# The latents' second FFN product as seven block products, with weight sums made by transfers that add into SBUF

## The chip, the cores and the metric

One core of one Trainium2 chip runs the whole program; seven cores are idle. The metric is the device time of one execution in microseconds (us), as the median of several runs. Engines are named as the profile names them: PE is TensorE (PEld its weight loads), DVE is VectorE, ACT is ScalarE, POOL is GpSimd, SP is SyncE, which only issues transfers here.

## The reference

Two layers of a diffusion backbone, on 1024 latent tokens and 256 context tokens of width 1024, in float32. Each layer has a mixer (attention on half of the heads, a spatial gate on the others) and then a SwiGLU FFN with 2816 hidden units:

```python
def swiglu(h, w_ffn_in, w_ffn_out):
    gate, up = jnp.split(h @ w_ffn_in, 2, axis=-1)
    return (jax.nn.silu(gate) * up) @ w_ffn_out
...
        fx = swiglu(modulate(rms_norm(x, g_pre_ffn[l]), mx[3], mx[4]), w_ffn_in[l], w_ffn_out[l])
        x = x + mx[5] * rms_norm(fx, g_post_ffn[l])
        if not last:
            fc = swiglu(modulate(rms_norm(xc, g_pre_ffn[l]), mc[3], mc[4]), w_ffn_in[l], w_ffn_out[l])
            xc = xc + mc[5] * rms_norm(fc, g_post_ffn[l])
```

The change concerns the last product of `swiglu` for the latents, (1024 x 2816) @ (2816 x 1024), in both layers. The vectors `mx` and `mc` come from six 1024 x 1024 products of the conditioning vectors with `w_mod` per layer.

## The kernel before, in words

A float32 product is made on PE as three products of float32r operands: each operand is split into a rounded part (`rnd`, an ACT copy) and a rest (`sub_lo`, a DVE subtraction of two SBUF operands), and high x high, high x low and low x high are summed in PSUM. So each 128 x 128 x 512 block of a product takes three matmuls and two splits that serve several blocks.

SBUF is handed out by rings: `PG` has 35 pages of 4 KB per partition, `BG` four buffers of 16 KB, `BK` the eight PSUM banks. Each engine works its instructions in a fixed order; the scheduler of the framework lays it down when the program is built, from the order of the code and from priorities.

For each layer, in order: projections of the mixer (`pz`, `pkv`, `pq`), attention, output projection (`op`), then the latents' FFN, then in layer 0 the context's FFN (`ffn`).

- `ffn_in` makes the latents' hidden units. It is already a product in seven block products (Strassen-Winograd): POOL makes the block sums of the weights (`wsplit`), each of the products takes 12 matmuls into one PSUM bank (`product`), DVE and ACT combine. Hidden units go to DRAM as 22 tiles `hid[j]` of 128 units x 1024 tokens.
- `ffn_out` is the product that changes. It takes the 22 tiles in chunks of two to four. For a chunk, SP loads `hid[j]` and row block j of `w_fo` (512 KB each) into `BG`, ACT and DVE split them (`foh`, `fol`, 128 x 1024), and then for each of eight token tiles and each half of the output columns PE does three matmuls per j. DVE adds the result of a chunk to `acc` (L1264); ACT copies the first chunk there. A generator loads and splits the next chunk meanwhile.
- `mods_steps` are small jobs that make `mx` and `mc`: per job 8 loads of 512 KB of `w_mod`, 8 (or 16, for both vectors) multiply-adds of 128 x 1024 on DVE (L234) into `macc`, and a few matmuls `mg`. `fill(n)` takes n steps of the queued jobs at places where DVE has room. In layer 0, nine such jobs (`later`) are queued before the FFN and are worked off in `ffn_in` and `ffn_out` of layer 0; layer 1 has none.
- `post` (L1346 on) is the end for a token tile: add the last partial sums (L1352), squares on ACT, `rsqrt` on POOL, scale on DVE (L1373), add the residual (L1374), store. In layer 1 it is called by `l_fin` for each token tile in the last chunk, and its last instance ends the program.

Of the kernel before, what the change touches and what calls it, by code (L numbers as in the profile page):

```python
# [10 lines left out]
F32 = mybir.dt.float32  # L11
F32R = mybir.dt.float32r
# [83 lines left out]
def trunk(ctx: ExitStack, tc, x, xctx, w_mod, b_mod, vecs, gqk, gsg, g_post, w_z, w_in, w_sT, w_out,  # L96
# [418 lines left out]
    def layer(l):  # L515
        nonlocal xl_d, xc_d
        last = l == DEPTH - 1
        hT = HT()
# [51 lines left out]
        for g, (kind, prs) in enumerate(groups):  # L570
            upages[g] = [PG.get([2 * len(prs), PC], F32, "u") for _ in range(2)]
            for k, pr in enumerate(prs):
# [634 lines left out]
        def ffn_out(done, hook, fills, chunks):  # L1207
            acc = []
            parts = {}
            starts = [sum(chunks[:i]) for i in range(len(chunks) + 1)]  # L1210

            def load(c):
                n = chunks[c]
                raws = []
                for k in range(2):
                    b = BG.get([n, 1024], F32, "fo")
                    raws.append(shares(b, [b.t[:, i] for i in range(n)]))
                    for i in range(n):
                        j = starts[c] + i
                        dma(out=b.t[:, i], in_=w_fo[l, j * P:(j + 1) * P, :] if k else hid[j])  # L1220
                parts[c] = []
                for i in range(n):
                    res = []
                    for k in range(2):
                        hi, lo = PG.get([1024], F32R, "foh"), PG.get([1024], F32R, "fol")
                        rnd(hi.t, raws[k][i].t)
                        sub_lo(lo.t, raws[k][i].t, hi.t)
                        raws[k][i].free()
                        res.append((hi, lo))
                    parts[c].append(res)  # L1230
                    yield

            def run():
                for c, n in enumerate(chunks):
                    first, final = c == 0, c == len(chunks) - 1
                    nxt = iter(()) if final else load(c + 1)
                    if first:
                        for _ in range(2):
                            b = BG.get([4, 1024], F32, "acc")
                            acc.extend(shares(b, [b.t[:, i] for i in range(4)]))  # L1240
                    if final:
                        hook()
                    for tt in range(NL):
                        if not final:
                            fill(fills)
                        sl = slice(tt * P, (tt + 1) * P)
                        bks = [BK.get([512], F32, "fo") for _ in range(2)]
                        for hs in (((0,), (1,)) if final and tt == NL - 1 else ((0, 1),)):
                            for i, ((hh, hl), (wh, wl)) in enumerate(parts[c]):
                                for k, (st_, mv) in enumerate(((hh, wh), (hh, wl), (hl, wh))):  # L1250
                                    for h in hs:
                                        mm(bks[h].t, st_.t[:, sl], mv.t[:, h * 512:(h + 1) * 512], i + k == 0,
                                           i == n - 1 and k == 2)
                        if tt > 0:
                            next(nxt, None)
                        if final:
                            done(tt, acc[tt], bks)
                            continue
# [275 lines left out]
```

## Time and profile before

| | |
|---|---|
| median of 3 runs | 2755.24 us (2754.25 to 2755.7) |
| the profiled execution's own time | 2754.34 us |
| its span (first to last instruction) | 2752.6 us, so 1.74 us lie around it |
| mean granted TensorE clock | 0.993 of full speed |
| PE busy | 2704.4 us, 98% |
| DVE, ACT, POOL busy | 72%, 45%, 16% |
| share of fo matmuls in the chain that ended last | 19.3% |

An engine's busy time is the time in which at least one of its instructions ran. Matmuls overlap in the pipeline, so the cost of one is read from the distance between starts, and not from its duration.

### The profile page before, as it was taken

To read this page: it belongs to the slowest core of one execution; us is meant where nothing else is said; L and a number is where in the kernel's file an instruction comes from. 1 tells how busy PE (TensorE), PEld (TensorE's weight loads), DVE (VectorE), ACT (ScalarE), POOL (GpSimd) and SP (SyncE) were. 2 spreads that over 40 slices of the span, in tenths; PEclk is the share of its full clock that TensorE was granted. 3 is DMA by queue.
4 is the path that set the end of the run, shared out by engine and by line. 5 is a ranking of instruction groups with operands and counts; after the bars stand their busy time and mean duration, and the time that the engine had idled before them with its cause. 6 is when DMAs were issued, how large, how long until landed. Compare 5 with 4: busy or idle time off the path is not lost.

```text
span 2752.6 us, 35200 instructions
## 1 busy us (share of the span) xinstructions
PE 2704.4 (98%) x13393; PEld 2216.6 (81%) x13393; DVE 1973.9 (72%) x2806; ACT 1234.4 (45%) x2073; POOL 435.6 (16%) x463
## 2 busy tenths in 40 slices
PE   7999999999999999999999999999998999999998
PEld 3789777688888788888899889777787888888887
DVE  6775878857888897865688556888758666666544
ACT  5323888845233223411276423788744333335111
POOL 1012000013233332000010002000013232330003
PEclk9999999999999999999999999999999999999999
DMA  7330000233532443742376410001232221225223
GB/s 283 123 117 32 9 10 26 78 111 108 210 128 107 153 144 132 257 170 98 105 240 224 146 56 32 5 9 39 93 126 92 85 80 66 92 77 191 85 77 115
DMA packets 91608, 298.04 MB, mean 108 GB/s; under 512 B 20431, under 2 KB 21263, under 8 KB 86318
## 3 DMA queue, kind: packets, MB, share of 16 engines
q1 hardware_dynamic: 91438, 295.78, 30.8%
q8 instruction: 105, 1.72, 0.3%
q14 instruction: 65, 0.53, 0.1%
HBM read 249.96 MB, written 45.71 MB: 107 GB/s over the span
## 4 chain that ended last, share of the span: by engine, by line
PE 88%; ACT 4%; DVE 3%; DMA 3%; issue 1%; POOL 1%; SPq 0%; DVEq 0%; POOLq 0%; ACTq 0%
PE fi_k L112 35%; PE fo_k L112 19%; PE op_k L112 7%; PE pz_k L112 6%; PE pv_k L112 6%; PE st_k L112 4%; PE pq_k L112 4%; PE pkv_k L112 2%; PE ml_k L112 2%; ACT pt_p L115 1%; ACT sp_b L118 1%; PE mg_k L112 1%; PE hT_k L334 1%; DMA wor_p<-in_w_out_dram 1%; PE m_k L112 1%
## 5 line engine op out<-in xcount | busy, mean ns | idle before, releaser
L112 PE MATMUL fi_k<-blk_p,fw_p 128*128 128x512 f32 x2640 | 608.6, 390 | 1.2 <-ACT blk_p L118 1.2
L112 PEld LDWEIGHTS fi_k<-blk_p,fw_p 128*128 128x128 f32 x2640 | 496.2, 188 | 106.3 <-ACT blk_p L118 2.1
L112 PE MATMUL pv_k<-sp_b,vt_p 128*128 128x512 f32 (+2 forms) x1008 | 277.6, 394 | 4.9 <-DVE sp_b L121 3.9
L118 ACT ACTIVATE fw_p<-fir_b 128x512 fp32r<-128x512 f32 x200 | 125.7, 631 | 317.6 <-PE fi_k L112 301.3
L112 PE MATMUL fi_k<-blk_b,fw_p 128*128 128x512 f32 x1056 | 251.0, 394 | 0.0
L112 PEld LDWEIGHTS fi_k<-blk_b,fw_p 128*128 128x128 f32 x1056 | 200.9, 191 | 42.3 <-DVE y_p L990 0.4
L286 POOL TENSOR_SCALAR rs<-ss 128x1 f32<-128x1 f32 x74 | 22.9, 309 | 1335.3 <-DVE ss L986 608.8
L121 DVE TENSOR_TENSOR sp_b<-pt_p,sp_b 128x1024 fp32r<-128x1024 f32 (+1 forms) x168 | 200.3, 1195 | 27.9 <-ACT sp_b L118 25.7
L112 PE MATMUL fo_k<-foh_p,foh_p 128*128 128x512 f32 x704 | 218.5, 390 | 0.0
L112 PE MATMUL fo_k<-fol_p,foh_p 128*128 128x512 f32 x704 | 218.0, 389 | 0.0
L112 PE MATMUL fo_k<-foh_p,fol_p 128*128 128x512 f32 x704 | 217.8, 389 | 0.0
L112 PEld LDWEIGHTS pv_k<-sp_b,vt_p 128*128 128x128 f32 (+1 forms) x1008 | 162.5, 170 | 63.0 <-DVE sp_b L121 11.0
L1264 DVE TENSOR_TENSOR acc_b<-fo_k,acc_b 128x512 f32<-128x512 f32 x176 | 113.1, 684 | 139.2 <-PE fo_k L112 139.1
L737 DVE TENSOR_REDUCE mx<-ml_k 128x1 f32<-128x512 f32 x256 | 168.0, 684 | 36.9 <-PE ml_k L112 36.3
L118 ACT ACTIVATE foh_p<-fo_b 128x1024 fp32r<-128x1024 f32 x88 | 90.8, 1060 | 226.9 <-PE fo_k L112 123.9
L115 ACT ACTIVATE pt_p<-st_k 128x512 f32<-128x512 f32 (+1 forms) x336 | 180.5, 590 | 14.4 <-PE st_k L112 13.3
L121 DVE TENSOR_TENSOR fw_p<-fir_b,fw_p 128x512 fp32r<-128x512 f32 x200 | 177.4, 887 | 11.8 <-ACT fw_p L118 9.6
L234 DVE SCALAR_TENSOR_TENSOR macc_p<-wm_p,cT,macc_p 128x1024 f32<-128x1024 f32 x128 | 171.8, 1357 | 13.7 <-DMA wm_p<-in_w_mod_dram 11.6
L118 ACT ACTIVATE sp_b<-pt_p 128x1024 fp32r<-128x1024 f32 (+1 forms) x168 | 175.8, 1047 | 1.7
L112 PE MATMUL pz_k<-winh_p,hTl_b 128*128 128x512 f32 x512 | 160.3, 391 | 1.0 <-DVE hTl_b L121 0.5
L112 PEld LDWEIGHTS fo_k<-foh_p,foh_p 128*128 128x128 f32 x704 | 131.8, 188 | 28.8 <-issue 0.9
L112 PEld LDWEIGHTS fo_k<-fol_p,foh_p 128*128 128x128 f32 x704 | 132.1, 188 | 27.7
(261 smaller groups left out, 5191.8 us busy)
## 6 DMA issues: line engine op xcount, KB each, us to landing
wm_p<-in_w_mod_dram SPq DMA_DIRECT2D x112, 512.0 KB
fir_b<-in_w_fi_dram SPq DMA_DIRECT2D x40, 1024.0 KB
fir_p<-in_w_fi_dram SPq DMA_DIRECT2D x52, 512.0 KB
hid<-hid_p SPq DMA_DIRECT2D x44, 512.0 KB
fo_b<-hid SPq DMA_DIRECT2D x44, 512.0 KB
fo_b<-in_w_fo_dram SPq DMA_DIRECT2D x44, 512.0 KB
for_p<-in_w_fo_dram SPq DMA_DIRECT2D x22, 512.0 KB
wraw_p<-in_w_z_dram SPq DMA_DIRECT2D x16, 512.0 KB
```

What stands on the lines that cost most here:

```text
L112: nc.tensor.matmul(o, lhsT, rhs, start=start, stop=stop)
L115: A.activation(out=o, in_=i, func=f, **kw)
L118: A.activation(out=o, in_=i, func=AF.Copy)
L121: V.tensor_tensor(out=o, in0=i, in1=hi.bitcast(F32), op=ALU.subtract)
L234: V.scalar_tensor_tensor(out=accs[v].t, in0=w.t, scalar=cT[:, v, kt:kt + 1], in1=accs[v].t, op0=ALU.mult, op1=ALU.add)
L286: nc.gpsimd.tensor_scalar(out=y, in0=src, scalar1=float(eps), scalar2=1.0, op0=ALU.add, op1=ALU.mult)
L334: nc.tensor.transpose(bk.t[:, k, :], xs.t[:, (4 * q + k) * P:(4 * q + k + 1) * P], idn)
L737: V.tensor_reduce(out=mx[:, b, i:i + 1], in_=bk.t, axis=AX.X, op=ALU.max)
L1264: V.tensor_tensor(out=a, in0=bks[h].t, in1=a, op=ALU.add)
```

## The change

`ffn_out` is written anew. Tokens are halved (512 each), output columns are halved (512 each), and the hidden tiles are halved by parity: `Hab` is token half a of the tiles `hid[2p + b - 1]`, and `Wab` is column half b of the row blocks 2p + a - 1 of `w_fo`, for p from 0 to 10. The product is made as seven block products, in the order 1, 2, 7, 6, 4, 5, 3. Each has 11 steps p, and a step is 4 token tiles x 3 matmuls into four PSUM banks. The operand of a step is split into pages `fs` (128 x 2 x 512). POOL makes the combinations of hidden blocks (`comb`, in products 7, 6, 5 and 3). The sums of weight blocks are made in place: a transfer issued by POOL (`nc.gpsimd.dma_start` with `accum_op`) adds a block from DRAM to the block that lies in SBUF (products 7, 6, 4 and 5). Preparation of a step runs `LEAD` = 6 steps ahead of its matmuls, sums are issued 4 steps ahead of the preparation, loads 7.

Two smaller edits come with it: the jobs (1, 2), (1, 3), (1, 4) of `w_mod` move from layer 0 to the mixer projections of layer 1, and (1, 5) to layer 1's FFN; and `post` adds only the banks that it is given, since half of the results are complete before. In layer 1, `post` of token tiles 4 to 7 runs after product 5, while product 3 is made.

```diff
     def layer(l):
         nonlocal xl_d, xc_d
         last = l == DEPTH - 1
+        jobs.extend(mods_steps(*a) for a in later[l][0])
...
-                    if kind == "l":
-                        fill(4)
+                if kind == "l":
+                    fill(4)
...
-                fill(0)
+                fill(2)
...
-        def ffn_out(done, hook, fills, chunks):
+        def ffn_out(done, hook):
...
+            steps = [(i, p) for i in (1, 2, 7, 6, 4, 5, 3) for p in range(NPR)]
...
+            needs = {1: ("H11", "W11"), 2: ("H12", "W21"), 7: ("H21", "W12"), 6: ("H22",), 4: (), 5: ("H11", "W11"),
+                     3: ("H12", "W22")}
+            sums = {7: ("W12", "W22"), 6: ("W12", "W11"), 4: ("W12", "W21"), 5: ("W11", "W12")}
...
+            def more_loads():
+                n = done_["prep"]
+                while todo_ and todo_[0][0] < n + AHEAD and (todo_[0][0] <= n or len(PG.queue) > 6):
+                    load()
+                while sums_ and sums_[0][0] < n + SUM and (sums_[0][1], sums_[0][3]) in raw:
+                    _, dst, src, p = sums_.pop(0)
+                    nc.gpsimd.dma_start(out=raw[dst, p].t, in_=block(src, p), accum_op=add_)
+
+            def comb(o, a, b, op):
+                nc.gpsimd.tensor_tensor(out=o.t, in0=a.t, in1=b.t, op=op)
...
+                for x_ in (h, w):
+                    t = PG.get([2, 512], F32R, "fs")
+                    rnd(t.t[:, 0], x_.t)
+                    sub_lo(t.t[:, 1], x_.t, t.t[:, 0])
+                    res.append(t)
...
+            def mms(bk, i, p, t):
+                h, w = split[i, p]
+                for k, (a, b) in enumerate(((0, 0), (0, 1), (1, 0))):
+                    mm(bk.t, h.t[:, a, t * P:(t + 1) * P], w.t[:, b], p + k == 0, p == NPR - 1 and k == 2)
...
+                    elif i == 6:
+                        V.tensor_tensor(out=z_, in0=bk.t, in1=z_, op=add_)
+                        V.tensor_tensor(out=x_, in0=bk.t, in1=x_, op=sub_)
...
-        if not last:
-            jobs.extend(mods_steps(*a) for a in later)
-        load_out, run_out = ffn_out(l_fin, before_c, 0 if last else 1, [2, 3, 3, 3, 3, 4, 4] if last else [2, 3, 3, 3, 3, 3, 2, 3])
+        jobs.extend(mods_steps(*a) for a in later[l][1])
+        c0, run_out = ffn_out(l_fin, before_c)
...
+    later = [((), [(0, 3, (1,)), (0, 4, (1,)), (0, 5, (0, 1)), (1, 0, (0, 1)), (1, 1, (0, 1))]),
+             ([(1, 2, (0,)), (1, 3, (0,)), (1, 4, (0,))], [(1, 5, (0,))])]
```

On POOL, the place between the last `wsplit` of layer 0's `ffn_in` and what follows. `fir` and `S` are weight tiles of `ffn_in`, `macc` the sums of a `w_mod` job, `rs` the `rsqrt` of a norm. Before:

```order
L1102 TENSOR_TENSOR fir_b_9076<-fir_b_9076 128x512
L1105 TENSOR_TENSOR fir_b_9076<-fir_b_9076,S_p_9451 128x512
L227 MEMSET macc_p_9726 128x1024
L227 MEMSET macc_p_10039 128x1024
L227 MEMSET macc_p_10388 128x1024
L286 TENSOR_SCALAR rs<-ss 128x1
```

After the change, where `fo` are raw blocks (DMA rows are the adding transfers, TENSOR_TENSOR rows the `comb`):

```order
L1106 TENSOR_TENSOR fir_b_9076<-fir_b_9076,S_p_9436 128x512
L1261 DMA fo_p_9903<-in_w_fo_dram 128x512 x2
L1261 DMA fo_p_9953<-in_w_fo_dram 128x512 x2
L1261 DMA fo_p_9996<-in_w_fo_dram 128x512
L1264 TENSOR_TENSOR fo_p_9901<-fo_b_9553,fo_p_9901 128x512 x2
L1261 DMA fo_p_9996<-in_w_fo_dram 128x512
L1261 DMA fo_p_10040<-in_w_fo_dram 128x512 x2
L1264 TENSOR_TENSOR fo_p_9951<-fo_b_9553,fo_p_9951 128x512 x2
L1261 DMA fo_p_10086<-in_w_fo_dram 128x512 x2
```

Three memsets gave way to a queue of adding transfers and combinations in turn; 44 of each stand there per layer, and a transfer that waits for its block holds up the combinations behind it.

On PE, the first instructions of layer 0's `ffn_out`. Before, two banks (column halves) and the tiles `foh`, `fol`; the numbers are those of buffers:

```order
L112 MATMUL fo_k711_9668<-foh_p739_9590,foh_p737_9586 128x512
L112 MATMUL fo_k712_9669<-foh_p739_9590,foh_p737_9586 128x512
L112 MATMUL fo_k711_9668<-fol_p740_9591,foh_p737_9586 128x512
L112 MATMUL fo_k712_9669<-fol_p740_9591,foh_p737_9586 128x512
L112 MATMUL fo_k711_9668<-foh_p739_9590,fol_p738_9587 128x512
```

After, four banks (token tiles), three matmuls each per step:

```order
L112 MATMUL fo_k711_9695<-fs_p729_9559,fs_p728_9556 128x512 x3
L112 MATMUL fo_k712_9696<-fs_p729_9559,fs_p728_9556 128x512 x3
L112 MATMUL fo_k713_9697<-fs_p729_9559,fs_p728_9556 128x512 x3
L112 MATMUL fo_k714_9698<-fs_p729_9559,fs_p728_9556 128x512 x3
L112 MATMUL fo_k711_9695<-fs_p731_9594,fs_p730_9591 128x512 x3
```

A new pair of `fs` pages is needed every 12 matmuls, and the banks change every 132.

On DVE, the place where layer 0 ends and layer 1's projections begin. `macc` and `wm` belong to the moved jobs, `acc` to the context's token tiles, `winl` are splits of the next projection weights. Before:

```order
L376 TENSOR_TENSOR winl_p1168_13738<-wraw_p1166_13735,winh_p1167_13737 128x1024
L1321 TENSOR_TENSOR acc_p908_11679<-fo_k945_13644,acc_p908_11679 128x512
L1321 TENSOR_TENSOR acc_p908_11679<-fo_k946_13645,acc_p908_11679 128x512
L376 TENSOR_TENSOR winl_p1165_13732<-wraw_p1163_13729,winh_p1164_13731 128x1024
L376 TENSOR_TENSOR winl_p1171_13744<-wraw_p1169_13741,winh_p1170_13743 128x1024
```

After:

```order
L234 SCALAR_TENSOR_TENSOR macc_p_13884<-wm_p_13956,cT,macc_p_13884 128x1024
L234 SCALAR_TENSOR_TENSOR macc_p_14085<-wm_p_14088,cT,macc_p_14085 128x1024
L234 SCALAR_TENSOR_TENSOR macc_p_13884<-wm_p_13959,cT,macc_p_13884 128x1024
L234 SCALAR_TENSOR_TENSOR macc_p_14085<-wm_p_14091,cT,macc_p_14085 128x1024
L234 SCALAR_TENSOR_TENSOR macc_p_13884<-wm_p_13962,cT,macc_p_13884 128x1024
L234 SCALAR_TENSOR_TENSOR macc_p_14085<-wm_p_14094,cT,macc_p_14085 128x1024
L234 SCALAR_TENSOR_TENSOR macc_p_14085<-wm_p_14097,cT,macc_p_14085 128x1024
L376 TENSOR_TENSOR winl_p_14103<-wraw_p_14100,winh_p_14102 128x1024
```

Of the 24 multiply-adds that moved to layer 1, the first twelve stand close together there (the last seven of them are shown), ahead of the splits `winl` of the gate's second projection and ahead of the two matmuls `mg` that PE reaches after 143 matmuls of the projection.

## Rows read from the trace of the kernel before

**Rows 1.** The page: span, busy time per engine, chain by engine.

```profile
span 2752.6 us, 35200 instructions
PE 2704.4 (98%) x13393; PEld 2216.6 (81%) x13393; DVE 1973.9 (72%) x2806; ACT 1234.4 (45%) x2073; POOL 435.6 (16%) x463
PE 88%; ACT 4%; DVE 3%; DMA 3%; issue 1%; POOL 1%; SPq 0%; DVEq 0%; POOLq 0%; ACTq 0%
```

**Rows 2.** Busy time in both FFN stages of each layer; instruction counts in brackets.

```profile
core 0: us, PE busy (x) PEld busy (x) DVE busy (x) ACT busy (x) POOL busy (x), PEclk, DMA share, GB/s
760.00:1109.00 349.00, 349.00 (x1560) 287.88 (x1559) 294.22 (x353) 106.75 (x174) 117.37 (x75) 0.99 0.38 133
1109.70:1358.60 248.90, 248.90 (x1113) 203.79 (x1112) 165.13 (x211) 59.35 (x69) 3.41 (x6) 1.00 0.42 152
1556.00:1700.00 144.00, 144.00 (x881) 129.18 (x880) 80.30 (x161) 46.23 (x97) 22.01 (x39) 1.00 0.16 54
2150.00:2504.00 354.00, 354.00 (x1564) 293.12 (x1563) 229.24 (x301) 115.81 (x185) 98.04 (x71) 1.00 0.22 84
2504.40:2744.00 239.60, 239.56 (x1057) 198.02 (x1056) 120.04 (x158) 57.90 (x85) 24.29 (x27) 1.00 0.33 120
```

**Rows 3.** The chain that ended last, layer 1's FFN: start, us, what.

```profile
2096.87 407.74 PE fi_k L112 x1797
2504.60 233.71 PE fo_k L112 x1031
```

**Rows 4.** PE's timeline at the step from `ffn_in` to `ffn_out`, layer 1.

```profile
2495.83 8.78 PE L112 MATMUL fi_k<-blk_p,fw_p 128*128 128x512 f32 x38
2504.44 0.62 PE L112 MATMUL fo_k<-foh_p,foh_p 128*128 128x512 f32 x2
2504.89 0.61 PE L112 MATMUL fo_k<-fol_p,foh_p 128*128 128x512 f32 x2
```

**Rows 5.** Groups by shape: busy us, mean ns, idle before and its releasers.

```profile
L118 ACT ACTIVATE fw_p<-fir_b 128x512 fp32r<-128x512 f32 x200 | 125.7, 631 | 317.6 <-PE fi_k L112 301.3 <-POOL fir_b L1102 6.6 <-DVE macc_p L234 4.2
L1264 DVE TENSOR_TENSOR acc_b<-fo_k,acc_b 128x512 f32<-128x512 f32 x176 | 113.1, 684 | 139.2 <-PE fo_k L112 139.1
L234 DVE SCALAR_TENSOR_TENSOR macc_p<-wm_p,cT,macc_p 128x1024 f32<-128x1024 f32 x128 | 171.8, 1357 | 13.7 <-DMA wm_p<-in_w_mod_dram 11.6 <-issue 1.2
L227 POOL MEMSET macc_p<- 128x1024 f32 x16 | 15.3, 954 | 147.4 <-DVE macc_p L234 55.2 <-PE fo_k L112 28.1 <-DVE winl_p L376 26.8
```

**Rows 6.** One tile's instructions: min/median/max ns (splits, POOL sums, SP issues).

```profile
L121 DVE TENSOR_TENSOR fw_p<-fir_b,fw_p x200: 673/692/1772, 705.2 to 2491.8; 128x512 fp32r<-128x512 f32 x100
L1100 POOL TENSOR_TENSOR S_p<-fir_b x40: 1277/1291/2225, 696.8 to 2471.3; 128x512 f32<-128x512 f32 x40
L1220 SPq DMA_DIRECT2D fo_b<-hid x44: 320/426/1396, 1059.6 to 2626.3; - x44
```

**Rows 7.** Timeline of DVE and POOL in layer 1's `ffn_in`.

```profile
2301.26 1.29 POOL L1101 TENSOR_TENSOR S_p<-S_p,fir_b 128x512 f32<-128x512 f32 x1
2301.36 1.74 DVE L121 TENSOR_TENSOR fw_p<-fir_b,fw_p 128x512 fp32r<-128x512 f32 x1
2302.51 1.75 POOL L1102 TENSOR_TENSOR fir_b<-fir_b 128x512 f32<-128x512 f32 x1
2303.03 1.78 DVE L1148 TENSOR_TENSOR hid_p<-hid_p,u_p 128x512 f32<-128x512 f32 x1
2304.73 0.68 DVE L1135 TENSOR_TENSOR u_p<-fi_k,u_p 128x512 f32<-128x512 f32 x1
2305.34 0.68 DVE L121 TENSOR_TENSOR fw_p<-fir_b,fw_p 128x512 fp32r<-128x512 f32 x1
```

**Rows 8.** Transfers: a busy stretch, and landings in the chain that ended last.

```profile
1120.00:1150.00 30.00, 30.00 (x134) 24.86 (x133) 26.68 (x25) 14.07 (x20) 1.91 (x2) 1.00 0.99 367
528.18 4.30 DMA wor_p<-in_w_out_dram
1540.84 6.23 DMA wraw_p<-in_w_z_dram
```

**Rows 9.** The end of the program: PE and DVE timeline.

```profile
2743.57 0.39 PE L112 MATMUL fo_k<-foh_p,fol_p 128*128 128x512 f32 x1
2744.19 0.68 DVE L1352 TENSOR_TENSOR acc_b<-fo_k,acc_b 128x512 f32<-128x512 f32 x1
2748.10 1.29 DVE L1374 TENSOR_TENSOR acc_b<-acc_b,x_p 128x512 f32<-128x512 f32 x2
```

More of the change, by code (lines that the diff above doesn't have):

```diff
@@ L1231, in load @@
                     yield
             def run():
[L1234 to L1241, printed above, removed]
-                        hook()
[L1243 to L1258, printed above, removed]
-                        for h in range(2):
-                            a = acc[tt].t[:, h * 512:(h + 1) * 512]
-                            if first:
-                                act(a, bks[h].t, AF.Copy)
-                            else:
-                                V.tensor_tensor(out=a, in0=bks[h].t, in1=a, op=ALU.add)
-                            bks[h].free()
-                    for _ in nxt:
-                        pass
-                    for res in parts.pop(c):
-                        for a in res:
-                            for b in a:
-                                b.free()
@@ L1273, in ffn_out @@
-            return load, run
+                for _ in range(2):
+                    b = BG.get([4, 1024], F32, "acc")
+                    acc.extend(shares(b, [b.t[:, k] for k in range(4)]))
+                half["acc"] = None
+                bks = None
+                for i, p in steps:
+                    more_loads()
+                    if ready_:
+                        prep()
+                    if (i, p) == ((4, 0) if last else (3, 0)):
+                        hook()
+                    if p == 0:
+                        bks = [BK.get([512], F32, "fo") for _ in range(4)]
+                    if i == 3 and p >= TM:
+                        if p == NPR - 1:
+                            for t in range(4):
+                                for q in range(TM, NPR):
+                                    mms(bks[t], 3, q, t)
+                                done(t, acc[t], [(1, bks[t])], t == 3)
+                            for q in range(TM, NPR):
+                                drop_split(3, q)
+                            if not last:
+                                for t in range(4, NL):
+                                    done(t, acc[t], [])
+                        continue
+                    for t in range(4):
+                        mms(bks[t], i, p, t)
+                    drop_split(i, p)
+                    if p == NPR - 1:
+                        evict(i, bks)
@@ L1275, in ffn @@
+            return begin(), run
         def ffn(h2v, T, done, cur, hook=None, tail=2, chores=()):
@@ L1351, in add @@
             def add(h):
-                V.tensor_tensor(out=acc.t[:, hs[h]], in0=bks[h].t, in1=acc.t[:, hs[h]], op=ALU.add)
-                bks[h].free()
+                for k, bk in bks:
+                    if k == h:
+                        V.tensor_tensor(out=acc.t[:, hs[h]], in0=bk.t, in1=acc.t[:, hs[h]], op=ALU.add)
+                        bk.free()
             if late:
@@ L1390, in layer, with l_fin @@
         chores, tails = [], []
-        def l_fin(tt, acc, bks):
+        def l_fin(tt, acc, bks, end=False):
             if last:
                 rest = post(acc, bks, xl_d[tt], cc["g_l"], out[tt * P:(tt + 1) * P, :],
-                            eng=V if tt == NL - 1 else nc.gpsimd)
+                            eng=V if end else nc.gpsimd)
                 next(rest)
@@ L1399, in l_fin @@
                 tails.append(rest)
-                if tt == NL - 1:
+                if end:
                     next(rest)
@@ L1426, in c_fin @@
         def c_fin(tt, acc, bks):
-            for _ in post(acc, bks, xc_d[tt], cc["g_c"], None):
+            for _ in post(acc, list(enumerate(bks)), xc_d[tt], cc["g_c"], None):
                 pass
@@ L1473, in trunk @@
         jobs.append(mods_steps(0, part, vs_))
-    later = [(0, 3, (1,)), (0, 4, (1,)), (0, 5, (0, 1)), (1, 0, (0, 1)), (1, 1, (0, 1)), (1, 2, (0,)), (1, 3, (0,)),
-             (1, 4, (0,)), (1, 5, (0,))]
+    later = [((), [(0, 3, (1,)), (0, 4, (1,)), (0, 5, (0, 1)), (1, 0, (0, 1)), (1, 1, (0, 1))]),
+             ([(1, 2, (0,)), (1, 3, (0,)), (1, 4, (0,))], [(1, 5, (0,))])]
     layer(0)
```

108 lines of the change are left out of this document (86 added, 22 removed).

## The prediction

> **What bounds the kernel now.** I read the page first: PE is busy for 98% of the span and holds 88% of the chain that ended last [rows 1]. An average says nothing of the stage that changes, so I then cut the span into stages. In both FFN stages of both layers PE is busy for the whole stretch at full clock: 248.90 of 248.90 us in layer 0's second product and 239.56 of 239.60 us in layer 1's, while DVE has work for 165 and 120 us and POOL for 3 and 24 us [rows 2]. The chain says the same: 233.71 us of it is one unbroken run of 1031 fo matmuls [rows 3]. So in this stage the end is set by the number of matmuls, and what is off PE has room.
>
> A matmul's own duration (0.39 us) is no price, since matmuls overlap. The price is the distance between starts: 38 matmuls from 2495.83 to 2504.44 make 0.2266 us each, two fo matmuls 0.45 us [rows 4]; the chain gives 233.71 / 1031 = 0.2267 us [rows 3]. The block products of `ffn_in` (the fi rows) have the loop that the change brings here (12 matmuls into a bank, a weight load for each), and they run at 407.74 / 1797 = 0.2269 us. The new loop therefore has the price of the old one.
>
> **What is removed.** Before, a layer has 22 tiles x 8 token tiles x 2 halves x 3 = 1056 matmuls. After, 7 products x 11 steps x 12 = 924. That is 132 fewer per layer and 264 in all: 264 x 0.2267 = 59.8 us. A step lasts 12 x 0.2267 = 2.72 us and the 77 steps of a layer 209.5 us. The matmuls `mg` of the four moved jobs are the same ones at another place where PE is also busy (the third of [rows 2]): 0. Layer 0's stage is 9.5 us longer than its 1056 matmuls (239.4 us); that is `mg` and transposes, which are kept or moved: 0.
>
> **What is added, per layer, against 209.5 us of PE.**
>
> ACT: two splits per step, 154 x 0.631 = 97 us [rows 5], and four copies. Hidden.
>
> DVE: 154 subtractions at the median 0.692 us [rows 6] = 106.6 us, and 28 additions from PSUM at 0.684 us [rows 5] = 19.2 us. Against this there is a collision: while POOL combines two SBUF tiles, a DVE instruction that reads two SBUF tiles takes 1.74 and 1.78 us in place of 0.68, and one that reads PSUM stays at 0.68 [rows 7]; the maximum of 200 splits is 1.772 us [rows 6]. So a combination holds up at most one such instruction by 1.08 us: 44 x 1.08 = 47.5 us at worst. Sum at most 173 us of 209.5. Hidden, and if this cover went (DVE over 209.5 us), every further us would be PE's.
>
> POOL: 44 combinations at 1.29 [rows 6] to 1.75 us [rows 7], say 1.5. And 44 adding transfers, of which no row exists. Their price on POOL is bounded below by what SP needs to issue a load, 0.43 us [rows 6], and above by POOL's shortest full-tile instruction, 0.954 us [rows 5], held up by three DVE instructions of 0.69 us, 3.03 us. I take 0.95, since it is POOL that must do the work and PSUM readers do not hold it. Is there time? The first sum is queued 4 steps ahead of preparation 22, when PE is at step 12; the last is for step 65, prepared when PE is at step 59. In those 47 steps (127.8 us) POOL has 33 combinations (49.5 us) and 44 sums. So 78.3 / 44 = 1.78 us per sum are free, and 2.15 us if the six steps of lead (16.3 us) are eaten too. At 0.95 us nothing waits.
>
> Landing: loads landed 4.30 to 6.23 us after issue for 512 KB [rows 8]. An adding transfer of 256 KB may take less, or twice that (12.5 us) if the add halves the rate. Four steps and six of lead allow 27.2 us. Hidden.
>
> Traffic: 121 loads and 44 sums of 256 KB are 43.3 MB in 209.5 us, 206 GB/s; with sums counted twice 262 GB/s. 367 GB/s were moved over 30 us [rows 8]. Hidden, if the short rows of 2 KB don't cost more than the 4 KB rows of that stretch.
>
> At one point a page speaks against this. First the row: only DVE instructions with two SBUF inputs were held, and by one POOL instruction each [rows 7]. The Trainium skill, page "SBUF — State Buffer", section "SBUF: two separate sides", calls the port pair that POOL and DVE share an exclusive lock, which a DVE instruction with two SBUF inputs takes only against a POOL instruction that reads SBUF; the trace agrees for combinations (1.74 us). By that rule the splits don't hold up the writing of descriptors, and the sum stays as it is. The same page tells of a transfer issued by POOL that took some 3.1 us in place of 0.62 beside a DVE copy in a two-port mode; if that held here, my estimate from its figure would be 44 x (3.1 - 2.15) = 42 us of waiting per layer, and the time about 2783. No run here shows it yet.
>
> **The moved jobs.** 24 multiply-adds of 1.357 us [rows 5] go to layer 1's projections, where DVE is busy for 80 of 144 us and PE for all of it [rows 2]. The first twelve (16.3 us) stand close together ahead of the first `mg`, which PE reaches after 143 matmuls, 32 us in. They fit, if their loads land; the context's last work and one landing of 6.23 us [rows 8] take most of the rest. Between 0 and 16.3 us; I take 2. What is late next would be the splits `winl`, which PE needs 43 us in.
>
> **The ends.** The last matmul starts at 2743.57 and the span ends 9 us later, through add, square, `rsqrt`, scale, add, store [rows 9]. This chain is kept. Four tiles are finished earlier, but the last four have 15 matmuls (3.4 us) each in place of 24, so POOL's residual adds come closer together: 1 us. For queueing between ACT, DVE and POOL around the changes of banks I take 2 us per layer.
>
> **Sum.** 2754.34 - 59.8 + 2 + 1 + 4 = 2701.5 against the profiled execution; the median is 0.9 us above that, so 2702.4, and I predict 2702. The floor is the bare removal, 2755.2 - 59.8 = 2695; a few us more if some small idle of layer 0 goes with the jobs.
>
> **Rivals.**
> - B, slower: POOL's issue is held out by DVE. The place is products 7 and 6, where each step has a combination and a sum. Price at 3.03 us per sum: 44 x (3.03 - 2.15) = 38.7 us of PE waiting per layer, 77.4 in all, so 2702 + 77 - 4 = 2775. It decides from (59.8 - 5) / 88 = 0.62 us above 2.15, at 2.8 us per sum. For it: no row shows an adding transfer, DVE is at work half of the time or more, and serial landings at 4.30 us each would do the same (189 us against 127.8 + 16.3 + 10.9 = 155). Against it: SP's issues overlap at 0.43 us, and PSUM readers aren't held.
> - C, a part is given back: in products 7 and 6 (59.9 us) DVE has 44 splits, 12 additions and 22 collisions, 30.4 + 8.2 + 23.8 = 62.4 us; if each sum holds up one instruction as well, 86.2 us. Less the lead, 10 us of PE waiting per layer, and up to 20 if a late sum stops ACT's fixed order. Time about 2727 (2713 to 2745). For it: 1.78 us in [rows 7]; against it: the mean of all such splits in that stage is far below its maximum (median 0.692 us).
> - D, the moved jobs stop PE in layer 1: all twelve, 16.3 us, 2718. For it: late loads; against it: DVE's 64 us of room.
>
> That the matmuls are not removed is no rival: their count stands in the instruction order.
>
> **Chances.** Forecast (2692 to 2712) 0.74, B 0.09, C 0.12, D 0.05. The range from 2691 to 2738 takes in the forecast, D and most of C. What a measurement can tell from no change is about 0.2%, 5.5 us. All but B end below 2749: faster 0.89, same 0.02, slower 0.09 (B beyond its point).
>
> **What would show it.** Right: 924 fo matmuls per layer at 0.227 us, stages of 211 to 219 us, PE busy throughout, POOL's sums near 1 us, splits between 0.69 and 1.78 us, POOL busy for 57 to 77 us per stage with its combinations. Wrong: PE idle before fo matmuls, released by DVE or ACT splits `fs` that wait for a POOL transfer (B, C), with sums over 2 us or landings over 27 us; PE idle before `mg` or `pz` in layer 1, released by `macc` or `winl` (D). Most of all the prediction hangs on the one price that has no row, the sum's.

## The result, and the profile after

The changed kernel took 2710.5 us (median of 4 runs, 2706.85 to 2716.43), the one before 2755.5 in the same comparison: a ratio of 0.9838, with a 95% interval from 0.9824 to 0.9852. That is 45 us less, where 53 were forecast; the range from 2691 to 2738 holds it. The profiled execution took 2710.63 us.

The page after, in the lines that answer to [rows 1]: span, busy time per engine, chain by engine.

```profile
span 2708.7 us, 35573 instructions
PE 2652.2 (98%) x13129; PEld 2174.4 (80%) x13129; DVE 2049.6 (76%) x2882; ACT 1304.0 (48%) x2269; POOL 640.1 (24%) x639
PE 85%; ACT 5%; DVE 4%; DMA 3%; issue 2%; POOL 1%; SPq 0%; POOLq 0%; DVEq 0%; ACTq 0%
```

PE has exactly the 264 matmuls fewer (13393 to 13129) and 52.2 us less to do. DVE has 76 instructions more, POOL 176. The stages of [rows 2] after the change, same columns: layer 0's second product, layer 1's projections, its first product, its second product.

```profile
1111.90:1330.60 218.70, 213.83 (x942) 176.50 (x941) 167.89 (x206) 89.75 (x156) 103.32 (x92) 0.98 0.74 194
1526.00:1670.00 144.00, 144.00 (x847) 127.03 (x847) 107.12 (x184) 44.63 (x90) 23.64 (x38) 0.99 0.40 136
2130.00:2486.00 356.00, 356.00 (x1567) 293.36 (x1566) 236.34 (x314) 121.16 (x199) 101.93 (x72) 1.00 0.26 96
2486.60:2695.80 209.20, 209.20 (x925) 173.26 (x923) 157.50 (x195) 88.81 (x170) 121.69 (x111) 1.00 0.78 209
```

The last row is the forecast come true: 924 matmuls, PE busy for all of the 209.2 us at full clock. The first is not: PE was idle for 4.9 us of 218.7, and the mean granted clock is 0.98.

Laid beside each other, the two profiled executions (2752.6 and 2708.7 us of span) differ by 43.8 us. Piece by piece, each counted from its first matmul's start to that of the next piece (differences taken before rounding):

| stretch | before | after | difference |
|---|---|---|---|
| start to layer 0's second product | 1109.7 | 1111.8 | +2.1 |
| layer 0's second product | 249.0 | 218.8 | -30.2 |
| from there to layer 1's z | 195.9 | 195.2 | -0.6 |
| layer 1's front, z to op | 422.4 | 430.6 | +8.2 |
| op and first product, layer 1 | 527.6 | 530.2 | +2.6 |
| layer 1's second product, to its last matmul's start | 239.1 | 209.2 | -29.9 |
| from there to the end | 9.0 | 12.9 | +4.0 |

Of the front's 8.2 us, 5.2 are `mg` matmuls that came with three of the moved jobs; of the first product's time 1.8 are those of the fourth. These 7 us left layer 0's second product. That stage should therefore have become some 37 us shorter and not 30. Against the 211.2 us that it takes where PE never waits (e11 below), 7.6 us are lost there, at one place. PE's timeline of the changed kernel:

```profile
1275.67 15.80 PE L112 MATMUL fo_k<-fs_p,fs_p 128*128 128x512 f32 x69
1294.40 1.15 PE L334 MATMUL hT_k<-idr,xs_p 128*128 128x128 f32 x8 [2.93 <-DVE xs_p L298]
1297.49 9.46 PE L112 MATMUL fo_k<-fs_p,fs_p 128*128 128x512 f32 x31 [1.94 <-DVE acc_b L1331]
1306.79 1.03 PE L334 MATMUL hT_k<-idr,xs_p 128*128 128x128 f32 x8
1307.58 23.17 PE L112 MATMUL fo_k<-fs_p,fs_p 128*128 128x512 f32 x101
```

`hT` is the transposes of the context, which `before_c` calls between products 5 and 3. They waited 2.93 us for their norm, the next product's banks 1.94 us for product 5's additions, and the 31 matmuls behind took 9.3 us from start to start instead of 7.0: the granted clock was 0.88 from 1280 to 1300 and 0.95 from 1300 to 1320 (between the levels 1.2 and 2.4 GHz), after PE had been idle. What was late shows in the chain that ended last, of that stretch (start, us, what):

```profile
1277.59 5.18 DVE fs_p L121 x3
...
1286.70 1.29 DVE fs_p L121 x2
1287.99 0.02 SPq L408
...
1288.05 3.41 DMA x_p<-xc
...
1293.59 0.04 DVE xs_p L298
```

The load of the context's tile (L408) was issued at 1288.05, 176.3 us into the stage, behind late splits, and the norm needs 6.3 us from there to its last step. The transposes come behind 792 matmuls, 179.5 us into the stage. Before the change the load was issued at 1299.94 for transposes at 1324.23, and the first tile's norm was ready 18 us early (1305.56 + 0.75):

```profile
1299.94 1.68 SPq L408 DMA_DIRECT2D x_p<-xc  x2
1305.56 0.75 DVE L298 TENSOR_SCALAR xs_p<-x_p,rs 128x1024 f32<-128x1024 f32 x1 [1.83 <-POOL rs L287]
```

Two things make the preparation of the blocks late. First, load, combination, sum and split follow one another, each in the fixed order of its engine. The chain again, while PE goes from product 6 to product 4; in it the load stands behind the stage's first 480 matmuls:

```profile
1111.95 108.81 PE fo_k L112 x480
...
1221.64 6.18 DMA fo_p<-hid
...
1228.62 0.81 POOL fo_p L1264
...
1229.86 5.82 DMA fo_p<-in_w_fo_dram
...
1235.76 0.64 ACT fs_p L118
```

Second, DVE and POOL in their timeline, while PE is in product 4 and the blocks of product 5 are prepared:

```profile
1250.23 1.58 POOL L1264 TENSOR_TENSOR fo_b<-fo_b,fo_p 128x512 f32<-128x512 f32 x1
1251.47 1.18 POOL L1261 DMA_DIRECT2D fo_b<-in_w_fo_dram  x1
1252.07 1.90 POOL L1264 TENSOR_TENSOR fo_b<-fo_b,fo_p 128x512 f32<-128x512 f32 x1
1252.51 5.07 DVE L121 TENSOR_TENSOR fs_p<-fo_b,fs_p 128x512 fp32r<-128x512 f32 x1 [3.99 <-ACT fs_p L118]
1253.31 1.50 POOL L1261 DMA_DIRECT2D fo_b<-in_w_fo_dram  x1
1253.92 2.21 POOL L1264 TENSOR_TENSOR fo_b<-fo_b,fo_p 128x512 f32<-128x512 f32 x1
```

One split takes 5.07 us in place of 0.68, while POOL goes on to work off combinations and sums without a gap. The row of the splits and that of most sums (min/median/max ns) put it in numbers: half of all are as quick as before, the slowest split takes 7.4 us, and a sum's issue has its median at 0.877 us.

```profile
L121 DVE TENSOR_TENSOR fs_p<-fo_p,fs_p x212: 676/682/7411, 1116.1 to 2682.3; 128x512 fp32r<-128x512 f32 x106
L1261 POOL DMA_DIRECT2D fo_p<-in_w_fo_dram x74: 857/877/2566, 1128.6 to 2630.4; - x74
```

The turn of combinations and sums is not needed for it. Of the 15 splits that took over 1.85 us, 14 began while POOL was at a sum's issue and had combinations right behind it, and three combinations in a row do as well:

```profile
1154.96 1.19 POOL L1261 DMA_DIRECT2D fo_p<-in_w_fo_dram  x1
1155.52 4.44 POOL L1264 TENSOR_TENSOR fo_p<-fo_b,fo_p 128x512 f32<-128x512 f32 x3
1155.65 4.88 DVE L121 TENSOR_TENSOR fs_p<-fo_p,fs_p 128x512 fp32r<-128x512 f32 x1 [0.76 <-ACT fs_p L118]
```

And a late split makes sums late in turn: POOL sat idle for 19.7 us, in 23 waits for a split, before issues of sums (both layers).

At the end of the program, DVE, ACT and POOL for one of the last tiles (the rows that answer to [rows 9]):

```profile
2693.36 1.42 DVE L1476 SCALAR_TENSOR_TENSOR acc_b<-acc_b,rs,G_p 128x512 f32<-128x512 f32 x2 [0.94 <-POOL rs L287]
2694.19 2.96 POOL L1477 TENSOR_TENSOR acc_b<-acc_b,x_p 128x512 f32<-128x512 f32 x2 [0.86 <-DVE acc_b L1476]
2694.69 0.69 DVE L1455 TENSOR_TENSOR acc_b<-fo_k,acc_b 128x512 f32<-128x512 f32 x1
...
2696.16 1.00 DVE L1471 TENSOR_TENSOR ss<-ss 128x1 f32<-128x1 f32 x1 [0.79 <-ACT sqj_p L115]
...
2698.11 1.42 DVE L1476 SCALAR_TENSOR_TENSOR acc_b<-acc_b,rs,G_p 128x512 f32<-128x512 f32 x2 [0.94 <-POOL rs L287]
```

From one scaling to the next a tile takes 4.75 us, its 15 matmuls 3.4 us, so the last four tiles fall behind PE: from the last matmul's start to the end it is 12.9 us, where it was 9.0.

### The profile page after: what moved, and what is told of

Read it like the earlier page. It is cut to its first block, busy times and chain, and to the rows that moved or that the text cites. A ratio compares the mean times of both kernels' runs of the same rounds, so it can differ in the third digit from the quotient of the medians.

```text
span 2708.7 us, 35573 instructions
## 1 busy us (share of the span) xinstructions
PE 2652.2 (98%) x13129; PEld 2174.4 (80%) x13129; DVE 2049.6 (76%) x2882; ACT 1304.0 (48%) x2269; POOL 640.1 (24%) x639
## 4 chain that ended last, share of the span: by engine, by line
PE 85%; ACT 5%; DVE 4%; DMA 3%; issue 2%; POOL 1%; SPq 0%; POOLq 0%; DVEq 0%; ACTq 0%
PE fi_k L112 35%; PE fo_k L112 15%; PE pz_k L112 7%; PE op_k L112 6%; PE pv_k L112 6%; PE pq_k L112 4%; PE st_k L112 4%; PE pkv_k L112 2%; PE ml_k L112 2%; ACT pt_p L115 1%; ACT sp_b L118 1%; PE mg_k L112 1%; PE hT_k L334 1%; DVE fs_p L121 1%; DMA wor_p<-in_w_out_dram 1%
## 5 line engine op out<-in xcount | busy, mean ns | idle before, releaser
L112 PE MATMUL fo_k<-fs_p,fs_p 128*128 128x512 f32 x1848 | 421.9, 390 | 1.9 <-DVE acc_b L1331 1.9
L112 PEld LDWEIGHTS fo_k<-fs_p,fs_p 128*128 128x128 f32 x1848 | 348.3, 189 | 74.7 <-issue 2.2
L121 DVE TENSOR_TENSOR fs_p<-fo_p,fs_p 128x512 fp32r<-128x512 f32 x212 | 200.1, 998 | 56.1 <-ACT fs_p L118 55.5
L286 POOL TENSOR_SCALAR rs<-ss 128x1 f32<-128x1 f32 x74 | 23.2, 314 | 905.1 <-DVE ss L987 611.2
L112 PEld LDWEIGHTS fi_k<-blk_b,fw_p 128*128 128x128 f32 x1056 | 201.8, 191 | 43.8 <-DVE y_p L991 1.5
L118 ACT ACTIVATE fs_p<-fo_p 128x512 fp32r<-128x512 f32 x212 | 120.5, 622 | 142.7 <-POOL fo_p L1264 46.4
L1101 POOL TENSOR_TENSOR S_p<-fir_b 128x512 f32<-128x512 f32 x40 | 58.1, 1452 | 377.1 <-issue 331.6
L112 PE MATMUL fi_k<-h2c_p,fih_p 128*128 128x256 f32 x704 | 128.0, 284 | 0.0
L112 PEld LDWEIGHTS pz_k<-winh_p,hTl_b 128*128 128x128 f32 x512 | 96.0, 188 | 25.2 <-issue 1.7
```

The source lines that it names most:

```text
L112: nc.tensor.matmul(o, lhsT, rhs, start=start, stop=stop)
L118: A.activation(out=o, in_=i, func=AF.Copy)
L121: V.tensor_tensor(out=o, in0=i, in1=hi.bitcast(F32), op=ALU.subtract)
L286: nc.gpsimd.tensor_scalar(out=y, in0=src, scalar1=float(eps), scalar2=1.0, op0=ALU.add, op1=ALU.mult)
L1101: tt_(out=sp.t[:, 0], in0=a21, in1=a22, op=ALU.add)
```

## Theory, rivals and experiments

Theory: combinations and sums together make the preparation late, by held splits and by sums in series; that delays the context's tile, and costs the 7.6 us. Rivals: the combinations alone do it (as [rows 7] had it), the sums alone, or only the place of the norm's call is bad. For the tail: DVE's small addition, POOL's queue, or a lag against PE. All times stand beside runs of the kernel before on the same chip. "Stage" is layer 0's second product and "tail" the time from the last matmul's start to the end, both of the profiled execution; its transposes included, that stage is 211.2 us when PE never waits.

| kernel | us | ratio, 95% | stage | tail |
|---|---|---|---|---|
| the change | 2710.5 | 0.9838 (0.9824-0.9852) | 218.8 | 12.9 |
| e1 norm before product 5's middle | 2716.9 | 0.9856 (0.9841-0.9871) | 225.7 | 13.0 |
| e2 addition with one input | 2710.8 | 0.9835 (0.9819-0.9850) | 218.9 | 12.5 |
| e3 no sums | 2704.8 | 0.9809 (0.9790-0.9827) | 211.2 | 12.9 |
| e4 no combinations | 2703.4 | 0.9808 (0.9793-0.9822) | 211.2 | 13.0 |
| e5 norm within product 3 | 2704.0 | 0.9815 (0.9801-0.9828) | 212.5 | 14.0 |
| e6 residual additions on DVE | 2709.8 | 0.9833 (0.9820-0.9847) | 218.5 | 11.7 |
| e7 combinations on DVE | 2703.9 | 0.9813 (0.9799-0.9826) | 214.8 | 13.4 |
| e8 seven pairs at the end | 2709.9 | 0.9832 (0.9817-0.9847) | 219.8 | 10.7 |
| e9 e7, norm later, seven pairs | 2704.2 | 0.9810 (0.9795-0.9825) | 211.2 | 8.9 |
| e10 jobs back in layer 0 | 2730.9 | 0.9902 (0.9886-0.9919) | 247.6 | 13.0 |
| e11 e5, e6 and e7 | 2699.8 | 0.9797 (0.9784-0.9810) | 211.2 | 12.4 |
| e12 e11 with six pairs | 2700.4 | 0.9799 (0.9785-0.9812) | 211.2 | 13.2 |

The intervals of e3, e5, e7 and e9 touch that of the change, so what these gain is read from the stage and not from the time alone; those of e4 (just), e11 and e12 lie apart from it.

**e1, the norm earlier.**

```diff
-                    if (i, p) == ((4, 0) if last else (3, 0)):
+                    if (i, p) == ((4, 0) if last else (5, 4)):
```

> The hook of layer 0 (the context's norm with 16 transposes, and the first loads of the context's FFN) moves from the start of product 3 to step 4 of product 5; nothing else changes. Theory: the changed kernel lost 4.9 us of PE idle there (2.9 us for the transposes, which waited for the norm, and 1.9 us for product 3's banks, since the transposes took the free banks and left it those of product 5) and some 2.5 us of lower clock behind it; in mid-product the four free banks come back in the same order and the norm is early. So no idle at that place, the stage 6 to 7 us shorter, 2703 to 2705 us. Rival: DVE's and POOL's queues are late in general in this stretch, and PE then waits at another place of products 5 and 3: 2708 to 2713 us.

The expectation failed: 2716.9. The wait for banks went, but the transposes now waited 12.86 us. The chain of that stretch gives the norm's input a longer way:

```profile
1273.15 7.11 DMA fo_b<-hid
...
1280.33 1.27 POOL fo_b L1264
...
1282.16 1.14 ACT xs_p L115 x2
```

ACT takes the norm's squares in a fixed order behind a split, which waited for a combination, which waited for a load. Earlier in the order is not earlier in time while the queues are late.

**e2, the tail's small addition.**

```diff
-            V.tensor_tensor(out=s1, in0=ss[:, 0:1], in1=ss[:, 1:2], op=ALU.add)
+            V.tensor_reduce(out=s1, in_=ss, axis=AX.X, op=ALU.add)
```

> In the last norm the sum of the two squares' halves is made by a reduction of one SBUF tile in place of an addition of two; the work is the same otherwise. Theory: at the end of the program this tiny addition was held for 0.85 us by POOL's residual addition in each of the last tiles (1.00 us in place of 0.16), in a loop of 4.75 us per tile that is longer than the tile's 15 matmuls (3.4 us), so the last tile came 3.3 us late. A reader of one tile is not held: the loop falls to 3.9 us, the end behind the last matmul from 12.9 to about 10 us, 2707 to 2708 us in all. Rival: the loop is set by DVE's fixed order (the addition from PSUM behind the scaling of the tile before): only the last 0.85 us go, 2709.7 us.

```profile
2697.97 2.93 POOL L1477 TENSOR_TENSOR acc_b<-acc_b,x_p 128x512 f32<-128x512 f32 x2 [0.86 <-DVE acc_b L1476]
2699.94 0.16 DVE L1471 TENSOR_REDUCE ss<-ss 128x1 f32<-128x2 f32 x1 [0.79 <-ACT sqj_p L115]
2700.87 0.18 POOL L286 TENSOR_SCALAR rs<-ss 128x1 f32<-128x1 f32 x1
2701.72 1.41 DVE L1476 SCALAR_TENSOR_TENSOR acc_b<-acc_b,rs,G_p 128x512 f32<-128x512 f32 x2 [1.63 <-POOL rs L287]
```

The addition now takes 0.16 us, and almost nothing is gained (0.4 us of the tail): the root L286 stands in POOL's queue behind the residual additions and starts when they end, 0.77 us after the addition. The held addition had covered a queue of nearly the same length.

**e3 and e4, one half of POOL's work each.** In e3 the line of the sum's `dma_start` is gone, in e4 that of the combination.

> Leaves out the 88 adding transfers, so that products 7, 6, 4 and 5 use weight blocks without their sums; everything else stands as it was. Theory: the sums are covered, as forecast: layer 1's stage stays at 209.5 us, layer 0's loses at most the wait for the context's norm, 2706 to 2711 us. Rival: sums and their landings hold up the splits and so PE: 2700 to 2704 us.

> Leaves out POOL's 88 combinations of hidden blocks, so that products 7, 6, 5 and 3 use blocks that are not combined; the sums by transfer stay. Theory: the splits then keep to 0.69 us (mean 1.00 before in the tile group), which shows that the combinations and not the sums hold them, and DVE's work falls by some 35 us per layer. PE gains only what the late norm of layer 0 cost, 2 to 4 us: 2706 to 2709 us. Rival: sums hold the splits too: the mean stays above 0.8 us.

The splits' rows (min/median/max ns), first e3, then e4:

```profile
L121 DVE TENSOR_TENSOR fs_p<-fo_p,fs_p x212: 675/687/1797, 1116.7 to 2677.6; 128x512 fp32r<-128x512 f32 x106
```

```profile
L121 DVE TENSOR_TENSOR fs_p<-fo_p,fs_p x212: 680/686/1776, 1113.3 to 2675.4; 128x512 fp32r<-128x512 f32 x106
```

With either half gone no split takes over 1.8 us, and the stage has no idle time. Both times lie below what was expected. So neither the combinations nor the sums do it alone, and both theories put down beforehand, that the sums are covered and that the combinations alone hold the splits, are out. In e3, where POOL has runs of combinations without a gap, DVE gets its turn between them:

```profile
1240.96 7.87 POOL L1263 TENSOR_TENSOR fo_b<-fo_b,fo_p 128x512 f32<-128x512 f32 x4 [7.57 <-DMA fo_b<-hid]
1244.27 1.70 DVE L121 TENSOR_TENSOR fs_p<-fo_b,fs_p 128x512 fp32r<-128x512 f32 x1 [1.24 <-ACT fs_p L118]
1246.13 1.55 DVE L121 TENSOR_TENSOR fs_p<-fo_b,fs_p 128x512 fp32r<-128x512 f32 x1 [0.16 <-ACT fs_p L118]
```

The issue of the context's tile, counted from the stage's first matmul, tells the sizes: 164.5 us in e4, 166.6 in e3, 176.3 in the change. It has to come by 173.2 (179.5 - 6.3), so e3 and e4 make it, and the change is 3.1 us late, which are the 2.93 us of the wait.

**e5, the norm later.**

```diff
-                    if (i, p) == ((4, 0) if last else (3, 0)):
+                    if (i, p) == ((4, 0) if last else (3, 4)):
```

> The context's norm and its sixteen transposes are called in the middle of the last product (at its fifth pair of hidden tiles) instead of at its first; nothing else is changed. If the 7.5 us that the first layer's stage loses come from the place of that call (the norm's chain on ACT, POOL and DVE must be done when the bank evictions of the product before are also due), the idle rows at the transposes shrink and the stage falls from 218.8 us to 211 to 214, the whole to 2703 to 2707 on this chip. If they come from DVE being late as such, the wait stands at the transposes wherever they are: some 3 to 10 us in front of them, and 2710 to 2716 as a whole.

2704.0: the splits are as slow as ever (up to 5.6 us), the stage is 212.5 us and the only wait in it 1.00 us at the second eight transposes. So late splits cost next to nothing by themselves; they cost where something short of time stands behind them. The first tile's load was issued earlier here (167.5 us into the stage), but that doesn't decide it: issued at 176.3, as in the change, its norm would still have been ready before its transposes at 190.4. The rival that DVE is late as such, wherever the call is, is out.

**e6, the tail's residual additions.**

```diff
-                            eng=V if end else nc.gpsimd)
+                            eng=V if tt < 4 else nc.gpsimd)
```

> The residual additions of the last four tiles run on DVE instead of POOL (three of the four tiles; the fourth has them there already). If POOL's queue sets the loop of 4.75 us per tile at the end (two additions of 2.96 us stand ahead of the next tile's reciprocal root), the loop falls to the 3.4 us that fifteen matmuls take, and the program ends 9 to 10 us behind its last matmul's start instead of 12.9: 2707 to 2709 on this chip. If DVE's own queue is the limit as well (four more additions of about 0.7 us between its steps), the loop stays above 4 us and the gain is under 1.5 us.

2709.8, no difference that can be told from the change. The loop fell only to 4.23 us, and the tail to 11.7. POOL no longer stands in the way; what is left is one serial round on DVE, ACT, DVE, POOL and DVE, since in DVE's order the next tile's addition stands behind the scaling of the one before (1.42 + 0.69 us), and square (0.72), sum (0.36 us late behind DVE's own residual addition), root and hand-overs make the rest.

**e7, the combinations on DVE.**

```diff
-                nc.gpsimd.tensor_tensor(out=o.t, in0=a.t, in1=b.t, op=op)
+                V.tensor_tensor(out=o.t, in0=a.t, in1=b.t, op=op)
```

> All 88 combinations of hidden blocks run on DVE instead of POOL; the sums' transfers are still issued by POOL. If a split is held up because combination and sum stand back to back in POOL's queue, no split takes over about 1.8 us any more, the 7.5 us of the first layer's stage go (stage about 211 us) and the time is 2702 to 2706 on this chip, although DVE gets 44 times 0.68 = 30 us more work in each layer. If DVE's plain load is what makes its queue late (about 168 of 209.5 us busy in the first layer's stage), the 30 us more bring it to the bound: idle time in front of matmuls in both layers' stages and a time above 2715.

```profile
1110.30:1325.10 214.80, 212.31 (x941) 174.94 (x940) 153.22 (x251) 89.89 (x157) 40.38 (x48) 1.00 0.75 197
2480.00:2689.50 209.50, 209.50 (x925) 173.19 (x923) 151.26 (x240) 88.85 (x171) 60.34 (x67) 1.00 0.78 209
```

DVE got 45 instructions more in each stage, and its busy time fell from 167.9 to 153.2 us and from 157.5 to 151.3: the held time was more than the work that took its place. No split is over 1.78 us, and the context's tile is issued 172.0 us into the stage, just in time. So of the change's lateness against e3 (9.7 us) 4.3 went with the held splits, and 5.4 remain when POOL only issues sums. What these 5.4 are is not shown: a landing in series (5.82 us in the chain above) would fit, but DVE also has the combinations here. Four waits of together 2.5 us are left, at the second transposes and the banks, and the time is 2703.9.

**e8 and e9, longer last tiles.** In e8 `TM = NPR - 7` in place of `NPR - 5`; e9 adds e7's edit and calls the norm at (3, 3).

> In the last product the last seven instead of five pairs of hidden tiles are taken tile by tile, so that each of the last four tiles has 21 instead of 15 matmuls (21 times 0.2267 = 4.76 us instead of 3.40); the same matmuls in another order. If the 12.9 us behind the last matmul's start are one tile's chain (9.0 before) plus three times what a tile's loop of 4.75 us lacks against its matmuls (three times 1.35 = 4.05), the tail falls to about 9 us and the time by some 4 us, to 2707 to 2708 on this chip. If the loop follows the matmuls instead (the tail is a fixed chain, only longer than before), the tail stays at 12 to 13 us and the time within 1 us of the change's.

> Three edits together: the 88 combinations on DVE, the context's norm called inside the last product, and seven pairs of hidden tiles tile by tile at the end. The parts are 7 us for the first layer's stage (the first two do the same work there, so that they do not add) and 4 us for the tail: 2699 to 2702 on this chip. If DVE is full with the combinations as well as the norm in one product, some idle time comes back in front of the transposes and it is 2702 to 2706.

The last tiles are where the splits run out of lead (PE's timeline of e9):

```profile
2676.68 1.66 PE L112 MATMUL fo_k<-fs_p,fs_p 128*128 128x512 f32 x5 [1.92 <-DVE fs_p L121]
2678.98 17.64 PE L112 MATMUL fo_k<-fs_p,fs_p 128*128 128x512 f32 x65 [0.65 <-DVE fs_p L121]
```

In e8 the same two waits are 0.42 and 0.85 us. Its tail fell to 10.7 us and not to 9: the last tile's addition still began 1.42 us behind the last matmul's start (0.62 before the change), and the small addition behind it was held again (0.97 us in place of 0.16). The tail of 8.9 us in e9 stands beside a slower PE: it had waited 2.57 us for splits and then took 17.64 us for 65 matmuls that take 14.9 at full clock (0.83 was granted from 2676.5 to 2697). What the tail gained was paid in front of it: e8's time missed what was expected, and e9's fell into the worse of its two ranges, with the waits at the splits and not at the transposes.

**e10, the jobs back.** The four moved jobs go to layer 0's list, with `fill(1)` at each step of `run`.

> The three modulation jobs of layer 1 that the change put into layer 1's front, and the fourth beside its first product, go back to layer 0: one step of them at each of the second product's steps, so that DVE gets 4 times 8 additions of 1.36 us = 43 us more in the first layer's stage. If the moved jobs cost what the ledger says (5.2 us of mg matmuls and 2.8 of idle time and clock in layer 1's front, 1.8 beside its first product), layer 1's windows get shorter by 8 to 10 us, and the first layer's stage longer by the same mg matmuls (about 7 us) and by what DVE is late then: it had some 168 of 209.5 us busy and would have 211, so 10 to 40 us more idle time, 2715 to 2745 as a whole. If DVE has more room than its busy time says (a good part of which is held time), the stage grows by 7 to 10 us only, and the whole is 2708 to 2714.

```profile
1203.56 3.57 PE L112 MATMUL mg_k<-ones,macc_p 128*128 128x1 f32 x16 [15.72 <-DVE macc_p L234]
```

2730.9: layer 0's stage is 28.8 us longer, with 15.72 us of waiting in front of one `mg`, and the way from it to layer 1's second product 8.1 us shorter. Against this placing of them the move was worth some 20 us; its price in layer 1 is these 8.1 us, of which 7 are the same `mg` matmuls.

**e11 and e12, together.** e11 has the edits of e5, e6 and e7; e12 also `TM = NPR - 6`.

> Combinations on DVE, the context's norm called at the fifth pair of the last product, and the last tiles' residual additions on DVE; five pairs tile by tile at the end, as in the change. The combinations on DVE alone gave 2703.9 with 1.5 us of waits for bank evictions and 1.0 at the transposes left, and the residual additions took about 1.5 us from the tail: 2700 to 2703 on this chip, below every kernel so far. If DVE is too full in the last product of either layer, the waits move to the splits, as with seven pairs at the end, and it is 2703 to 2706.

> As the kernel before it in this call, with six instead of five pairs of hidden tiles tile by tile: 18 matmuls (4.08 us) against a tile's loop of 4.23 us. If the tail's lag is what the loop lacks against the matmuls, it is 3 times 0.15 instead of 3 times 0.83 us, 2 us less than with five; if the splits of six pairs come too late for the first of the last tiles (with seven pairs PE waited 0.42 and 0.85 us for them, and 1.92 and 0.65 with the combinations on DVE as well), the same or up to 4 us more.

Layer 0's and layer 1's second product in e11:

```profile
1112.10:1323.30 211.20, 211.20 (x941) 175.12 (x940) 153.05 (x250) 90.16 (x156) 40.33 (x48) 1.00 0.76 201
2480.60:2689.80 209.20, 209.20 (x925) 173.19 (x923) 151.26 (x242) 88.14 (x169) 55.95 (x64) 1.00 0.78 209
```

PE never waits in either stage any more, and with 2699.8 us e11 beats both kernels: 55 us under the kernel before and some 11 under the change. Six pairs (2700.4) don't differ from five in time, and the tail, which should have become 2 us shorter, is 13.2 us in place of 12.4; so the lag against the matmuls doesn't explain all of the tail, and the rest stays open. The profile of e11 is of its slowest run (2703.97), so where its other runs are a few us better can't be read.

## Why the prediction was right, and which steps of it were not

- **The removal.** 264 x 0.2267 = 59.8 us was right to the step: the new loop has the old one's price, and layer 1's stage lost 29.9 us.
- **The sum's price.** 0.95 us was taken from between 0.43 and 3.03; the median is 0.877, and 0.872 in e7 (at most 1.60), where POOL has no combinations. Landings: 3.7 to 10.9 us, median 6.3 for the 74 of the row above, with 27.2 allowed. Traffic: 209 GB/s, 206 forecast. Rival B had no place to start; the 3.1 us of the page "SBUF — State Buffer" of the Trainium skill (section "SBUF: two separate sides") and the 2783 that it led to came in no run as a price for every sum. That the splits don't hold up the writing of descriptors, as the forecast read from the same section, agrees with e7, where DVE had splits and combinations beside the issues. Among POOL's own combinations an issue took up to 2.57 us (1256.98), most of it while DVE was idle (1257.58 to 1259.88).
- **The steps that failed** are two "hidden". "A combination holds up at most one such instruction by 1.08 us" was read from [rows 7], where combinations stand alone; beside sums one split was held for 5.07 us here and for 7.4 at most. And "four steps and six of lead allow 27.2 us" for a landing was reckoned for the products alone, and PE indeed waited for no split; but a landing stands in series with whatever waits in the queues behind its split, here the context's load. DVE's total stayed below the forecast's 173 us (168 and 158), so "hidden" was right as a sum and wrong as a schedule. What suffered was not the products but the context's norm, with 18 us to spare before and none after. The 2 us for queueing were 7.6 in layer 0, and 0 in layer 1, where no norm of the context stands in the stage. Two of the forecast's own signs stayed out: splits up to 1.78 us, and POOL busy for 57 to 77 us per stage; it was busy for 103 and 122.
- **A row read for more than it shows.** That a DVE instruction reading PSUM "stays at 0.68" beside a combination isn't in [rows 7]: the one shown begins at 2304.73, behind the combination's end (2304.26). It is true all the same: in that kernel 47 such additions of 128x512 ran beside a POOL combination for over 0.6 us and took 0.67 to 0.69.
- **Rival C** had the right engines and the wrong victim: not the products' own matmuls, but the transposes behind them, for 7.6 us in one layer, less than the 11 us from which its range began.
- **The moved jobs** cost 3.0 us net in the front (2 forecast), and e10 shows what they would have cost in layer 0. Rival D did not happen.
- **The ends.** "Residual adds come closer together: 1 us" was 4.0. The mechanism was named, but not summed: a round of 4.75 us against 3.4 us of matmuls. The last tile's addition began 3.66 us behind the last matmul's start in place of 0.62, which makes 3.0 us, and its small addition was held for 0.8.

Together: queueing +5.6 and -2, the ends +3.0, the moved jobs +1.0, and 2.3 in stretches that the sum left alone (+2.1, -0.6, +0.8) make 9.9 us. Less 0.8 us, by which the old stage in layer 0 was longer than its matmuls, `mg` and transposes (249.0 against 248.2), this is the 9.1 between 2701.5 and the profiled 2710.63. e11 shows that the loss in layer 0 was no part of the idea: without it the time is 2699.8. Open is also whether more pages in SBUF would have done alone: the load of the chain above waited for PE's matmuls, and no run changed the number of pages. What stays open besides is a spread of several us between executions of one kernel: single stretches have a lower granted clock in one execution and not in the next (0.93 from 1700 to 1750 in e5's, 1.00 in e7's), and differences of 2 or 3 us between the kernels here are not told apart.

## What to carry to other kernels

When a stage is compressed, ask which side chain in it had slack and has none now; here the 7.6 us were lost by a norm of two tiles, not by the 924 matmuls. A queue that mixes two kinds of work is not priced by rows in which each stands alone: look at what a second engine gets between them, or move one kind away, even to the busier engine. And a step earlier in program order is only earlier in time if the queues that carry it are on time.

## What the runs showed of the hardware

Beside POOL's combinations alone a split took at most 1.80 us (99 splits, e3), so DVE got its turn between them; beside issues of sums alone it took at most 0.69 us (92 splits, e4). Where a split began while POOL was at a sum's issue, with combinations right behind it, it took over 1.85 us in 14 of 25 cases of the change, and 2.95 or more in ten of them (4.88 us behind three combinations, 5.07 and 7.41 us beside combinations and issues in turn). Why the two together do this, and why not always, no run here shows. It works both ways: a combination took 3.29 us at 1246.39, while DVE worked off the last of ten splits in a row (1242.42 to 1248.52). And an addition of 128x1 took 1.00 us in place of 0.16 beside POOL's residual additions, so here the number of SBUF inputs and not the size counts: the form with one input took 0.16 there (e2).
